# Layer A's attention: the transposes of the probabilities one step ahead of their products with the values

## The chip, the cores and the metric

The kernel runs on one core of a Trainium2 chip. The metric is the device time of one execution in microseconds (us), the median of several runs. The engines are TensorE (PE, with its weight loads as PEld), VectorE (DVE), ScalarE (ACT), GpSimd (POOL) and SyncE (SP), whose queue issues the DMAs here.

## What is computed

A trunk of two layers over 1024 positions of width 1024, in float32. Layer A is sparse attention: an indexer scores the keys, the 256 best admissible ones count, and 16 heads share one key and one value head. Then comes a squared-ReLU MLP, then layer B (latent attention) and a second MLP. The change touches layer A's attention alone. In the reference it is:

```python
def block(args):
    ...
    _, idx = lax.top_k(score, n_top)
    valid = (idx // CHUNK) <= t_chunk[None, :, None]
    kg = jax.vmap(lambda kk, ii: kk[ii])(k, idx)
    vg = jax.vmap(lambda vv, ii: vv[ii])(v, idx)
    logits = jnp.einsum('bqhd,bqkd->bhqk', qb, kg).astype(jnp.float32) * (A_HEAD_DIM ** -0.5)
    bias = rel_bias[t5_bucket(idx - t[None, :, None])]
    logits = logits + jnp.transpose(bias, (0, 3, 1, 2)).astype(jnp.float32)
    logits = jnp.where(valid[:, None], logits, NEG)
    p = jax.nn.softmax(logits, axis=-1).astype(vg.dtype)
    return jnp.einsum('bhqk,bqkd->bqhd', p, vg)
...
return out @ w_o
```

The kernel gathers nothing: it takes the logits of all admissible keys and adds a mask that is very negative where a key was not chosen.

## The kernel before

Positions are cut into eight blocks of 128, tb 0 to 7. `attend_a` runs twice, for the blocks (1, 3, 0, 2) at about 205 to 400 us and for (7, 4, 5, 6) at about 763 to 972 us. The first half of layer A's MLP lies between the two, its second half behind the second; layer B's attention follows at about 1345 to 1890 us, the last MLP to the end. Float32 products are made of two or three products of high and low parts (`split_evac`, line 88: ACT copies a PSUM tile to the high part, DVE or POOL subtracts it from the source for the low part).

A call's work is cut into units, one for a block and two heads (g, 0 to 7), 32 to a call. A unit has these steps:

- `logits` for each head (line 543: `lps`, two products per stretch of keys). Once a unit, SP loads the bias near the diagonal (`bm`, line 529, two buffers) and POOL adds the mask (line 530). DVE moves the logits to SBUF (`lg`), adds bias or mask and takes the running extreme (line 548, `sm`), ACT takes the exponential (552), DVE the reciprocal (553), POOL scales (554).
- `values` for two key blocks at a time: PE turns the probabilities (line 566, four transposes into a `ppt` tile), ACT and DVE split them into `ph` and `pl` (line 88), and PE multiplies those with the values `vv` into `po` (line 572). For each `ph`, `pl` and `ppt` there are two buffers in the first call; `ppt` has three in the second.
- `output`: ACT and DVE bring `po` to `res` (580 to 584).

Beside the units run: query projections (`pq`, line 185, blocks of 48 products), the query split and transposes (`qt`, `ptq`, line 515), the loading of the output weight (`load_wo`: eight times one DMA `wor_a`, ACT's `woh_a`, POOL's `wol_a`; a single `wor_a` buffer), and the output projections of the blocks that are done (`pwoa`, line 1066, two blocks of 24 products each, in a single PSUM buffer `pwo`; their residual add, line 1068).

The loop over k interleaves unit k's logits (`first`) with unit k-1's values (`second`), one step of each by turns, and strews the side work (`extra`) between; side work is tied behind the last transpose written before it (`self.anchor`). This program order is only a priority. A scheduler works out each engine's instruction order from it and from the buffers, and the engines then run their own lists strictly in that order.

Of the kernel before, what the change touches and what calls it, by code (L numbers as in the profile page):

```python
# [10 lines left out]
F32 = mybir.dt.float32  # L11
F32R = mybir.dt.float32r
# [6 lines left out]
P = 128  # L19
# [8 lines left out]
def woven(main, extra):  # L28

    steps, done = [], 0  # L30
    for i, step in enumerate(main):
        upto = (i + 1) * len(extra) // len(main)
        steps += [step] + extra[done:upto]
        done = upto
    return steps


def weave(main, extra, run=lambda e: e()):
    for step in woven(main, [lambda e=e: run(e) for e in extra]):
        step()  # L40


class Trunk:
# [433 lines left out]
    def attend_a(self, tbs, res, kh, kl, vv, score, edge, near_d, wst, lp=None, start=None, beside=None, free=None):  # L477
# [3 lines left out]
        nc, tc = self.nc, self.tc  # L481
        H, G = 16, 2
        wide = (max(tbs) + 1) * P
        nm0 = f"{tbs[0]}"
        with ExitStack() as st:
            qp = st.enter_context(tc.tile_pool(name="atq" + nm0, bufs=2))
            pp = st.enter_context(tc.tile_pool(name="atp" + nm0, bufs=2, space=PSUM))
            lp = lp or st.enter_context(tc.tile_pool(name="atl" + nm0, bufs=2, space=PSUM))
            queries, probs, outs = {}, {}, {}
# [30 lines left out]
            t2 = st.enter_context(tc.tile_pool(name="at2" + nm0, bufs=2))  # L520

            def logits(tb, g, i):
# [31 lines left out]
                nc.gpsimd.tensor_scalar(lg[:, :S], lg[:, :S], rs, 1.0, op0=ALU.mult, op1=ALU.mult)  # L554
                ps_h.append(lg)

            def values(tb, g, s0):
                nb = tb + 1
                if s0 == 0:
                    outs[tb, g] = pp.tile([P, G * P], F32, name=f"po{tb}_{g}", tag="po", bufs=2 if wide > 512 else 1)  # L560
                po, ps_h = outs[tb, g], probs[tb, g][2]
                ns = min(2, nb - s0)
                pt = pp.tile([P, 2, G, P], F32, name=f"ppt{tb}_{g}_{s0}", tag="pt", bufs=3 if wide > 512 else 2)
                for u in range(ns):
                    for i in range(G):
                        self.anchor = nc.tensor.transpose(pt[:, u, i], ps_h[i][:, (s0 + u) * P:(s0 + u + 1) * P], self.ident)  # L566
                ph = t2.tile([P, 2, G * P], F32R, name=f"ph{tb}_{g}_{s0}", tag="ph")
                pl = t2.tile([P, 2, G * P], F32R, name=f"pl{tb}_{g}_{s0}", tag="pl")
                self.split_evac(ph[:, :ns], pl[:, :ns], pt[:, :ns].rearrange("p u a b -> p u (a b)"))
                for u in range(ns):  # L570
                    for n, m in enumerate((ph, pl)):
                        nc.tensor.matmul(po, vv[:, s0 + u], m[:, u], start=(s0 + u == 0 and n == 0),  # L572
                                         stop=(s0 + u == nb - 1 and n == 1))

            def output(tb, g):

                po = outs.pop((tb, g))
                del probs[tb, g]
                of = t2.tile([P, P], F32, name=f"of{tb}_{g}", tag="of")
                nc.scalar.copy(of[0:64], po[64:128, 0:P])  # L580
                nc.scalar.copy(of[64:128], po[0:64, P:2 * P])
                dst = res[:, tb, g * P:(g + 1) * P]
                nc.vector.tensor_add(dst[0:64], po[0:64, 0:P], of[0:64])
                nc.vector.tensor_add(dst[64:128], po[64:128, P:2 * P], of[64:128])
# [6 lines left out]
            units = [(tb, g) for tb in tbs for g in range(H // G)]  # L591
            NU = len(units)

            def spread(steps, u0, u1):
                for n in range(u0, u1):
                    work[n] += steps[(n - u0) * len(steps) // (u1 - u0):(n - u0 + 1) * len(steps) // (u1 - u0)]


            work = [[] for _ in units]
# [7 lines left out]
            for k in range(NU + 1):  # L607
                if k == n0 + 1:
                    if free:
                        free()  # L610
                    wop = wst.enter_context(tc.tile_pool(name="awo" + nm0, bufs=1, side="right"))
                    wo, load = self.load_wo(wop, t1, self.d["a_w_o"][0], "a" + nm0)
                    spread(load, n0, n1)
                first = [lambda i=i: logits(*units[k], i) for i in range(G)] if k < NU else []
                second, extra = [], []
                if k:
                    tb, g = units[k - 1]
                    second = [lambda s0=s0: values(tb, g, s0) for s0 in range(0, tb + 1, 2)] + [lambda: output(tb, g)]
                    m = (k - 1 - n1) // each
                    if k > n1 and (k - 1 - n1) % each == 0 and m < 3:  # L620
                        spread(project(tbs[m]), k - 1, k - 1 + each)
                    extra = work[k - 1]
                steps = []
                for i in range(max(len(first), len(second))):
                    steps += second[i:i + 1] + first[i:i + 1]
                weave(steps, extra, self.behind)
            self.anchor = None

        def finish(tb, split, bank):
# [629 lines left out]
```

## Time and profile before

| | us |
|---|---|
| median of three runs | 2685.81 (2684.93 to 2688.6) |
| the profiled execution | 2684.85 |
| its span, first to last instruction | 2683.0 |
| PE busy within the span | 2532.4 |

The profiled execution lies 1 us below the median; 1.9 us of it are outside the span. Its mean granted clock is 0.984 of full speed. An engine's idle time is listed under what ended it, so a wait named "po <- DVE pl" is PE standing at a values product until DVE's subtraction was done.

### The profile page before, as it was taken

To read this page: it belongs to the slowest core of one execution; us is meant where nothing else is said; L and a number is where in the kernel's file an instruction comes from. 1 tells how busy PE (TensorE), PEld (TensorE's weight loads), DVE (VectorE), ACT (ScalarE), POOL (GpSimd) and SP (SyncE) were. 2 spreads that over 40 slices of the span, in tenths; PEclk is the share of its full clock that TensorE was granted. 3 is DMA by queue.
4 is the path that set the end of the run, shared out by engine and by line. 5 is a ranking of instruction groups with operands and counts; after the bars stand their busy time and mean duration, and the time that the engine had idled before them with its cause. 6 is when DMAs were issued, how large, how long until landed. Compare 5 with 4: busy or idle time off the path is not lost.

```text
span 2683.0 us, 36853 instructions
## 1 busy us (share of the span) xinstructions
PE 2532.4 (94%) x13354; PEld 2148.5 (80%) x13354; DVE 1521.1 (57%) x3655; ACT 1232.2 (46%) x2989; POOL 1024.1 (38%) x756
## 2 busy tenths in 40 slices
PE   6997799999989999999998999998999999999999
PEld 5897678888768888888888788887778888888887
DVE  5798754999869861222257878897422232222223
ACT  4575744333357764243345777787222222222221
POOL 2235635443556535343324555555121212222120
PEclk9998999999999999999999999999999999999999
DMA  7202323222232223233210000002210101111111
GB/s 157 54 24 60 99 92 97 94 99 90 79 110 68 60 82 127 84 120 106 77 33 11 10 14 10 14 5 80 102 32 32 63 32 63 47 48 48 48 47 63
DMA packets 122293, 173.03 MB, mean 64 GB/s; under 512 B 12752, under 2 KB 101104, under 8 KB 122112
## 3 DMA queue, kind: packets, MB, share of 16 engines
q1 hardware_dynamic: 122112, 170.69, 20.5%
q8 instruction: 105, 1.72, 0.3%
q14 instruction: 76, 0.62, 0.1%
HBM read 159.13 MB, written 11.53 MB: 64 GB/s over the span
## 4 chain that ended last, share of the span: by engine, by line
PE 71%; DVE 7%; DMA 3%; ACT 3%; POOL 2%; issue 2%; SPq 0%; POOLq 0%; DVEq 0%; ACTq 0%
PE pd L1190 25%; PE pu L1120 25%; PE pwo L1066 3%; PE pwoa L1066 2%; PE blps L938 2%; PE bpo L962 2%; PE puq L794 2%; PE po L572 1%; PE ppt L566 1%; PE lps L543 1%; PE pcq L853 1%; PE pukv L750 1%; DVE bpr L939 1%; PE bpt L957 1%; PE pck L853 1%
## 5 line engine op out<-in xcount | busy, mean ns | idle before, releaser
L88 POOL TENSOR_TENSOR dl<-rd,dh 128x1024 fp32r<-128x1024 f32 x96 | 232.4, 2429 | 728.2 <-PE pu L1120 369.3
L1191 DVE TENSOR_TENSOR res<-res,pd 128x1024 f32<-128x1024 f32 x192 | 234.2, 1220 | 419.1 <-PE pd L1190 419.1
L1120 PE MATMUL pu<-mxh,uh 128*128 128x512 f32 (+1 forms) x1056 | 405.4, 384 | 2.4 <-DVE mxl L88 2.4
L1120 PE MATMUL pu<-mxl,uh 128*128 128x512 f32 (+1 forms) x1056 | 404.9, 383 | 0.0
L1120 PE MATMUL pu<-mxh,ul 128*128 128x512 f32 (+1 forms) x1056 | 404.9, 383 | 0.0
L1190 PE MATMUL pd<-dh,hh 128*128 128x512 f32 x1024 | 398.6, 390 | 5.1 <-DVE res L1191 3.1
L1190 PE MATMUL pd<-dl,hh 128*128 128x512 f32 x1024 | 398.5, 389 | 0.0
L1190 PE MATMUL pd<-dh,hl 128*128 128x512 f32 x1024 | 392.9, 389 | 1.6 <-DVE hl L88 1.6
L88 DVE TENSOR_TENSOR hl<-pu,hh 128x512 fp32r<-128x512 f32 (+1 forms) x132 | 88.8, 674 | 407.6 <-ACT hh L88 407.6
L88 ACT CAST dh<-rd 128x1024 fp32r<-128x1024 f32 x96 | 99.1, 1051 | 476.1 <-PE pd L1190 422.5
L88 POOL TENSOR_TENSOR ul<-ru,uh 128x1024 fp32r<-128x1024 f32 x96 | 231.9, 2418 | 167.2 <-ACT uh L88 166.9
L1177 ACT ACTIVATE pu<-pu 128x512 f32<-128x512 f32 (+1 forms) x132 | 75.0, 569 | 433.2 <-PE pu L1120 427.7
L1120 PEld LDWEIGHTS pu<-mxh,uh 128*128 128x128 f32 x1056 | 199.1, 189 | 41.7 <-DVE mxl L88 2.9
L1120 PEld LDWEIGHTS pu<-mxl,uh 128*128 128x128 f32 x1056 | 198.9, 188 | 39.0
L1120 PEld LDWEIGHTS pu<-mxh,ul 128*128 128x128 f32 x1056 | 199.0, 188 | 38.7
L1190 PEld LDWEIGHTS pd<-dh,hh 128*128 128x128 f32 x1024 | 192.3, 188 | 46.5 <-DVE res L1191 4.0
L1190 PEld LDWEIGHTS pd<-dh,hl 128*128 128x128 f32 x1024 | 192.2, 188 | 42.1 <-DVE hl L88 2.2
L1190 PEld LDWEIGHTS pd<-dl,hh 128*128 128x128 f32 x1024 | 192.3, 188 | 39.7
L444 DVE TENSOR_SCALAR_CACHE_REDUCE both<-score,cand 128x1024 f32<-128x1024 f32 (+1 forms) x192 | 181.2, 944 | 5.0
L944 POOL TENSOR_SCALAR bpr<-bpr,bsm 128x640 f32<-128x640 f32 (+7 forms) x128 | 98.4, 772 | 96.4 <-DVE bsm L943 55.9
L554 POOL TENSOR_SCALAR lg<-lg,sm 128x256 f32<-128x256 f32 (+7 forms) x128 | 99.4, 783 | 76.7 <-DVE sm L553 54.0
L88 ACT CAST uh<-ru 128x1024 fp32r<-128x1024 f32 x96 | 99.9, 1044 | 30.4 <-DMA ru<-in_mlp_w_up_dram 28.4
(374 smaller groups left out, 5982.0 us busy)
## 6 DMA issues: line engine op xcount, KB each, us to landing
ru<-in_mlp_w_up_dram SPq DMA_DIRECT2D x48, 1024.0 KB, 5.4
rd<-in_mlp_w_down_dram SPq DMA_DIRECT2D x48, 1024.0 KB, 4.9
bm<-near_d SPq DMA_DIRECT2D x56, 256.0 KB, 2.7
res<-in_x_dram SPq DMA_DIRECT2D x16, 512.0 KB, 6.3
wor_a<-in_a_w_o_dram SPq DMA_DIRECT2D x16, 512.0 KB, 3.6
wr_q<-in_a_w_in_dram SPq DMA_DIRECT2D x8, 512.0 KB, 8.7
x<-res SPq DMA_DIRECT2D x8, 512.0 KB, 2.6
wor_b<-in_b_w_o_dram SPq DMA_DIRECT2D x8, 512.0 KB, 3.6
```

What stands on the lines that cost most here:

```text
L88: return self.nc.scalar.copy(h, src), (engine or self.nc.vector).tensor_sub(l, src, h)
L444: nc.vector.tensor_scalar(scratch[0][0][:, :s.shape[-1]], s, cand[:, j:j + 1], None, op0=ALU.is_ge, op1=ALU.add, accum_out=cnt[:, j:j + 1])
L554: nc.gpsimd.tensor_scalar(lg[:, :S], lg[:, :S], rs, 1.0, op0=ALU.mult, op1=ALU.mult)
L794: nc.tensor.matmul(ps[:, 192 * u:192 * u + 192], a[:, kb, tsl], b[:, kb], start=(kb == 0 and i == 0), stop=(kb == 2 and i == 2))
L853: nc.tensor.matmul(ps, a[:, kb], b[:, kb], start=(kb == 0 and i == 0), stop=(kb == KB - 1 and i == 2))
L938: nc.tensor.matmul(lps, q[0:rows, tsl], k[0:rows, h, c:c + a], start=(m == 0), stop=(m == 2))
L944: nc.gpsimd.tensor_scalar(pr, pr, sm[:, 3:4], 1.0, op0=ALU.mult, op1=ALU.mult)
L1066: nc.tensor.matmul(open_ps[n], x[:, kb], w[:, kb, ns], start=(kb == 0 and i == 0), stop=(kb == KB - 1 and i == 2))
L1120: nc.tensor.matmul(pu, a[:, kb], b[:, kb, c0:c1], start=(kb == 0 and i == 0), stop=(kb == KB - 1 and i == 2))
L1177: nc.scalar.activation(pu, pu, AF.Relu)
L1190: nc.tensor.matmul(pd[:, ns], a[:, tsl], b[:, ns], start=(f == 0 and k == 0), stop=(f == NS - 1 and k == 2))
L1191: nc.vector.tensor_add(res[:, tb], res[:, tb], pd)
```

## The change

`values` is cut in two. The new `turn_probs` makes the transposes and the split; `values` keeps the products. For a unit the order is now: the first transposes; then, for each step, the next step's transposes, a share of the following unit's logits with the side work between them, and the products of this step; the output last. `ph` and `pl` get three buffers each instead of two. The number of instructions is the same, and so is the work of each.

```diff
--- before.py
+++ after.py
@@ -554,21 +554,28 @@
                 nc.gpsimd.tensor_scalar(lg[:, :S], lg[:, :S], rs, 1.0, op0=ALU.mult, op1=ALU.mult)
                 ps_h.append(lg)
 
+            parts = {}
+
+            def turn_probs(tb, g, s0):
+                ps_h = probs[tb, g][2]
+                ns = min(2, tb + 1 - s0)
+                pt = pp.tile([P, 2, G, P], F32, name=f"ppt{tb}_{g}_{s0}", tag="pt", bufs=3 if wide > 512 else 2)
+                for u in range(ns):
+                    for i in range(G):
+                        self.anchor = nc.tensor.transpose(pt[:, u, i], ps_h[i][:, (s0 + u) * P:(s0 + u + 1) * P], self.ident)
+                ph = t2.tile([P, 2, G * P], F32R, name=f"ph{tb}_{g}_{s0}", tag="ph", bufs=3)
+                pl = t2.tile([P, 2, G * P], F32R, name=f"pl{tb}_{g}_{s0}", tag="pl", bufs=3)
+                self.split_evac(ph[:, :ns], pl[:, :ns], pt[:, :ns].rearrange("p u a b -> p u (a b)"))
+                parts[tb, g, s0] = ph, pl
+
             def values(tb, g, s0):
                 nb = tb + 1
                 if s0 == 0:
                     outs[tb, g] = pp.tile([P, G * P], F32, name=f"po{tb}_{g}", tag="po", bufs=2 if wide > 512 else 1)
-                po, ps_h = outs[tb, g], probs[tb, g][2]
-                ns = min(2, nb - s0)
-                pt = pp.tile([P, 2, G, P], F32, name=f"ppt{tb}_{g}_{s0}", tag="pt", bufs=3 if wide > 512 else 2)
-                for u in range(ns):
-                    for i in range(G):
-                        self.anchor = nc.tensor.transpose(pt[:, u, i], ps_h[i][:, (s0 + u) * P:(s0 + u + 1) * P], self.ident)
-                ph = t2.tile([P, 2, G * P], F32R, name=f"ph{tb}_{g}_{s0}", tag="ph")
-                pl = t2.tile([P, 2, G * P], F32R, name=f"pl{tb}_{g}_{s0}", tag="pl")
-                self.split_evac(ph[:, :ns], pl[:, :ns], pt[:, :ns].rearrange("p u a b -> p u (a b)"))
-                for u in range(ns):
-                    for n, m in enumerate((ph, pl)):
+                po = outs[tb, g]
+                hl = parts.pop((tb, g, s0))
+                for u in range(min(2, nb - s0)):
+                    for n, m in enumerate(hl):
                         nc.tensor.matmul(po, vv[:, s0 + u], m[:, u], start=(s0 + u == 0 and n == 0),
                                          stop=(s0 + u == nb - 1 and n == 1))
 
@@ -611,19 +618,25 @@
                     wop = wst.enter_context(tc.tile_pool(name="awo" + nm0, bufs=1, side="right"))
                     wo, load = self.load_wo(wop, t1, self.d["a_w_o"][0], "a" + nm0)
                     spread(load, n0, n1)
-                first = [lambda i=i: logits(*units[k], i) for i in range(G)] if k < NU else []
-                second, extra = [], []
+                other = [lambda i=i: logits(*units[k], i) for i in range(G)] if k < NU else []
                 if k:
                     tb, g = units[k - 1]
-                    second = [lambda s0=s0: values(tb, g, s0) for s0 in range(0, tb + 1, 2)] + [lambda: output(tb, g)]
                     m = (k - 1 - n1) // each
                     if k > n1 and (k - 1 - n1) % each == 0 and m < 3:
                         spread(project(tbs[m]), k - 1, k - 1 + each)
-                    extra = work[k - 1]
-                steps = []
-                for i in range(max(len(first), len(second))):
-                    steps += second[i:i + 1] + first[i:i + 1]
-                weave(steps, extra, self.behind)
+                    other = woven(other or [lambda: None], [lambda e=e: self.behind(e) for e in work[k - 1]])
+
+                    starts = list(range(0, tb + 1, 2))
+                    n = len(starts)
+                    steps = [lambda: turn_probs(tb, g, 0)]
+                    for i in range(n):
+                        if i + 1 < n:
+                            steps += [lambda s0=starts[i + 1]: turn_probs(tb, g, s0)]
+                        steps += other[i * len(other) // n:(i + 1) * len(other) // n]
+                        steps += [lambda s0=starts[i]: values(tb, g, s0)]
+                    other = steps + [lambda: output(tb, g)]
+                for step in other:
+                    step()
             self.anchor = None
 
         def finish(tb, split, bank):
```

The scheduler's lists differ in the first call from about 259 us on, in the whole second call, and also in layer B's attention, whose code is untouched; both MLPs stand as before. Three places follow. The names are those of the last section; digits behind a name are block and unit or head, then the first key block.

PE in the first call, at the query projection `pq3_6` of 48 products. Before:

```order
L572 MATMUL po3_1_3037<-ph3_1_2_3069,vv_75 128x256
L572 MATMUL po3_1_3037<-pl3_1_2_3070,vv_75 128x256
L185 MATMUL pq3_6_2847<-wh_q3_1970,axh1_105 128x256
L185 MATMUL pq3_6_2847<-wl_q3_1969,axh1_105 128x256
L185 MATMUL pq3_6_2847<-wh_q3_1970,axl1_107 128x256
```

and in the change:

```order
L565 MATMUL ppt3_3_0_3153<-ident_58,lg3_6_3117 128x128
L565 MATMUL ppt3_3_0_3153<-ident_58,lg3_7_3131 128x128
L543 MATMUL lps3_13_0_3322<-kh_73,qst3_2722 128x512
L543 MATMUL lps3_13_0_3322<-kl_74,qst3_2722 128x512
L185 MATMUL pq3_6_2854<-wh_q3_1970,axh1_105 128x256
L185 MATMUL pq3_6_2854<-wl_q3_1969,axh1_105 128x256
L185 MATMUL pq3_6_2854<-wh_q3_1970,axl1_107 128x256
```

Half a unit's transposes and one head's logits (`lps3_13`) now stand ahead of the projection, where they stood behind it. At the projection before, `pq3_4`, `lps3_8` moved the other way, from ahead of it to behind.

POOL in the first call, at the fourth of the eight `wol_a`. Before:

```order
L530 TENSOR_TENSOR bm0_4_3606<-bm0_4_3606,edge_83 128x2x128
L88 TENSOR_TENSOR wol_a1_2981<-wor_a1_3_3281,woh_a1_2982 128x1024
L554 TENSOR_SCALAR lg0_5_3531<-lg0_5_3531,sm0_2_3517 128x128
L554 TENSOR_SCALAR lg0_6_3562<-lg0_6_3562,sm0_3_3561 128x128
L554 TENSOR_SCALAR lg0_7_3582<-lg0_7_3582,sm0_3_3561 128x128
L530 TENSOR_TENSOR bm0_5_3666<-bm0_5_3666,edge_83 128x2x128
L554 TENSOR_SCALAR lg0_8_3610<-lg0_8_3610,sm0_4_3609 128x128
```

and in the change:

```order
L554 TENSOR_SCALAR lg0_3_3484<-lg0_3_3484,sm0_1_3475 128x128
L554 TENSOR_SCALAR lg0_4_3515<-lg0_4_3515,sm0_2_3514 128x128
L554 TENSOR_SCALAR lg0_5_3523<-lg0_5_3523,sm0_2_3514 128x128
L554 TENSOR_SCALAR lg0_6_3556<-lg0_6_3556,sm0_3_3555 128x128
L530 TENSOR_TENSOR bm0_4_3600<-bm0_4_3600,edge_83 128x2x128
L554 TENSOR_SCALAR lg0_7_3571<-lg0_7_3571,sm0_3_3555 128x128
L530 TENSOR_TENSOR bm0_5_3647<-bm0_5_3647,edge_83 128x2x128
L88 TENSOR_TENSOR wol_a1_2981<-wor_a1_3_3272,woh_a1_2982 128x1024
L554 TENSOR_SCALAR lg0_8_3604<-lg0_8_3604,sm0_4_3603 128x128
```

`wol_a` stands behind the scaling of heads 5 to 7 and the mask of `bm0_5`, which it stood ahead of. The others but the first move the same way by one to four instructions, the last by three (`lg2_8`, `lg2_9`, `bm2_6`). On SP, `wor_a` number 1, 2 and 4 to 7 (counted from 0) stand behind one or two more `bm` loads: the seventh behind `bm2_4`, the eighth behind `bm2_6`, which stood behind them before. On PE the last steps of `pwoa1_0`, the projection that takes up the weight as it arrives, have six transposes (`ppt2_4`), six products (`po2_3`) and one head's logits (`lps2_15`) ahead of them that stood behind them. At the call's end the last unit's products `po2_7` stand ahead of 48 `pwoa0` and 38 MLP products (`pwo`), where they stood right ahead of the transposes `pt_m` that need their result. Three `res` loads, where two did, stand ahead of the first MLP weight on SP.

DVE in the second call, at the query split of block 5. Before:

```order
L88 TENSOR_TENSOR qt5_8156<-res_69,qt5_8156 128x16x64
L88 TENSOR_TENSOR pl7_5_4_7612<-ppt7_5_4_7606,ph7_5_4_7611 128x512
L548 ISA lg4_0_7751,sm4_0_7750<-lps4_0_384_7756,bm4_0_7747,sm4_0_7750 128x256
L548 ISA sm4_0_7750 128x1
L88 TENSOR_TENSOR pl7_5_6_7625<-ppt7_5_6_7619,ph7_5_6_7624 128x512
```

and in the change:

```order
L88 TENSOR_TENSOR pl7_5_4_7583<-ppt7_5_4_7577,ph7_5_4_7582 128x512
L548 ISA lg4_0_7769,sm4_0_7768<-lps4_0_0_7770,score4_79 128x384
L548 ISA sm4_0_7768 128x1
L553 RECIPROCAL sm7_7_7676<-sm7_7_7676 128x1
L548 ISA lg4_0_7769,sm4_0_7768<-lps4_0_384_7774,bm4_0_7765,sm4_0_7768 128x256
L548 ISA sm4_0_7768 128x1
L88 TENSOR_TENSOR qt5_8172<-res_69,qt5_8172 128x16x64
L548 ISA lg4_1_7794,sm4_0_7768<-lps4_1_0_7795,score4_79 128x384
L548 ISA sm4_0_7768 128x1
L88 TENSOR_TENSOR pl7_5_6_7608<-ppt7_5_6_7602,ph7_5_6_7607 128x512
```

`pl7_5_4`, which the next values product needs, stands six instructions ahead of `qt5`; before it stood right behind. In several units of block 5 the transposes of three tiles now follow one another on PE, with up to six `pwoa` products behind them; before, four transposes and three `pwoa` took turns. Over the second call's PE list a transpose is followed by something else 130 times, before 123 times.

## Rows read from the trace of the kernel before

**Rows 1.** The page's busy time of each engine, share of the span, instructions.

```profile
PE 2532.4 (94%) x13354; PEld 2148.5 (80%) x13354; DVE 1521.1 (57%) x3655; ACT 1232.2 (46%) x2989; POOL 1024.1 (38%) x756
```

**Rows 2.** Stretches: us; PE, PEld, DVE, ACT, POOL busy (instructions); PE clock; DMA share, GB/s.

```profile
270.00:350.00 80.00, 61.05 (x377) 49.63 (x377) 60.01 (x244) 57.32 (x157) 58.26 (x64) 0.96 0.35 103
330.00:350.00 20.00, 15.14 (x82) 11.00 (x83) 15.84 (x70) 15.05 (x42) 18.81 (x20) 1.00 0.44 132
350.00:400.00 50.00, 47.40 (x239) 38.78 (x238) 25.27 (x65) 20.05 (x43) 10.16 (x10) 1.00 0.22 76
763.00:820.00 57.00, 47.19 (x291) 38.61 (x290) 50.65 (x160) 44.39 (x80) 44.55 (x32) 0.94 0.35 104
820.00:970.00 150.00, 145.64 (x986) 131.12 (x985) 133.17 (x416) 110.16 (x242) 77.45 (x72) 1.00 0.18 50
1445.00:1890.00 445.00, 404.81 (x2614) 347.41 (x2611) 364.80 (x1117) 337.04 (x1097) 242.68 (x254) 0.97 0.07 21
```

**Rows 3.** PE's waits, 259 to 400 us: line <- releaser: total us, times, longest.

```profile
PE lps L543 <- DVE sm L548: 4.4, 4, 1.9
PE po L572 <- DVE pl L88: 2.6, 4, 1.1
PE ptq L515 <- DVE pl L88: 2.1, 1, 2.1
PE ppt L566 <- DVE pl L88: 1.6, 4, 1.1
PE pt_m L116 <- DVE res L584: 1.3, 1, 1.3
```

**Rows 4.** Timeline, loading of the output weight: start us, us, engine, line, operation [idle before].

```profile
287.10 2.39 POOL L88 TENSOR_TENSOR wol_a<-wor_a,woh_a 128x1024 fp32r<-128x1024 f32 x1
330.42 0.35 SPq L1045 DMA_DIRECT2D wor_a<-in_a_w_o_dram  x1
334.15 1.04 ACT L88 CAST woh_a<-wor_a 128x1024 fp32r<-128x1024 f32 x1 [0.65 <-DMA wor_a<-in_a_w_o_dram]
336.91 2.39 POOL L88 TENSOR_TENSOR wol_a<-wor_a,woh_a 128x1024 fp32r<-128x1024 f32 x1
344.10 2.41 POOL L88 TENSOR_TENSOR wol_a<-wor_a,woh_a 128x1024 fp32r<-128x1024 f32 x1
344.60 3.38 SPq L529 DMA_DIRECT2D bm<-near_d  x2
```

**Rows 5.** Groups of 290 to 400 us: count | busy us, mean ns | idle before.

```profile
L88 DVE TENSOR_TENSOR pl<-ppt,ph 128x512 fp32r<-128x512 f32 x16 | 10.9, 688 | 2.1 <-ACT ph L88 2.0
L88 ACT CAST ph<-ppt 128x512 fp32r<-128x512 f32 x15 | 8.7, 582 | 5.9 <-PE po L572 4.3 <-PE ppt L566 1.5
```

**Rows 6.** Timeline around DVE's query splits (columns as in rows 4).

```profile
813.83 2.38 POOL L88 TENSOR_TENSOR wol_a<-wor_a,woh_a 128x1024 fp32r<-128x1024 f32 x1
814.39 2.90 DVE L88 TENSOR_TENSOR qt<-res,qt 128x1024 fp32r<-128x1024 f32 x1
817.94 0.39 PE L572 MATMUL po<-pl,vv 128*128 128x256 f32 x1 [2.66 <-DVE pl L88]
302.86 1.22 DVE L88 TENSOR_TENSOR qt<-res,qt 128x1024 fp32r<-128x1024 f32 x1
304.26 2.38 POOL L88 TENSOR_TENSOR wol_a<-wor_a,woh_a 128x1024 fp32r<-128x1024 f32 x1 [2.28 <-ACT woh_a L88]
```

**Rows 7.** Timeline of PE in the second call: successive instructions.

```profile
866.31 0.29 PE L572 MATMUL po<-pl,vv 128*128 128x256 f32 x1
866.43 0.60 PE L566 MATMUL ppt<-ident,lg 128*128 128x128 f32 x4
866.79 0.48 PE L1066 MATMUL pwoa<-woh_a,oh 128*128 128x512 f32 x1
867.11 0.40 PE L1066 MATMUL pwoa<-wol_a,oh 128*128 128x512 f32 x1
867.34 0.40 PE L1066 MATMUL pwoa<-woh_a,ol 128*128 128x512 f32 x1
```

## The prediction, made before the changed kernel ran

> **What bounds the kernel now.** I read the page's busy times first, then the stretches of the two calls, then PE's waits in the part that the order changes, and last the timeline of what those waits hang on. PE is busy 94% of the span [rows 1], so only PE's idle time within the changed stretches can be won, and no more than that. The second call has little of it: from 820 to 970 us PE is busy 145.64 of 150 us and DVE 133.17; only its start, 763 to 820 us, stands 57 - 47.19 = 9.8 us, part of it the entry that the change does not touch. The first call has more: 80 - 61.05 = 19 us from 270 to 350 us, while from 350 to 400 us PE runs almost without a gap (47.40 of 50). From 330 to 350 us POOL is the fullest, 18.81 of 20 us [rows 2]. So there are two regimes in the first call: up to about 348 us PE waits for others, behind it PE sets the end.
>
> The waits from 259 us on are of two kinds. Those that the change aims at end with DVE's `pl`: at a product 2.6 us, at a turned query 2.1 (one wait), at a probability transpose 1.6, together 6.3 us. The others, 4.4 us at the logits alone, end with DVE's reduction [rows 3]. The split that PE waits for takes 0.58 us on ACT and then 0.69 on DVE [rows 5]; a transpose group followed at once by its products pays both.
>
> What sets the point where PE becomes dense is the output weight. A step of its loading took 334.15 - 330.42 = 3.73 us from issue to ACT, 1.04 on ACT and 2.39 on POOL, 7.16 together; the single `wor_a` buffer lets the next begin only then. The eight ran from 287.10 to 344.10 us, 57.0/7 = 8.14 us apart [rows 4]. Only with the last one can the first projection's half finish its sums, and since the projections share one PSUM buffer, all that follows is PE work that waits for nothing else.
>
> **The change part by part.** No instruction is added; what moves is counted here, against the profiled execution (2684.85 us, span 2683.0). It lies 0.96 us under the median, so I add the difference to the median, 2685.81.
>
> *First call, lead of the attention.* With the transposes a step ahead, the next transposes and logits lie between a split and its products, and half a unit stands ahead of the 48-product block `pq3_6`, so ACT, DVE and POOL have work during it. I count half of the 6.3 us as gone, 3.15, because in the same lists `lps3_8` moved behind a block of that length, and since a shorter wait for `pl` shows the one for the logits behind it. The bounds are 0 and 6.3. Moving the last `wol_a` behind `bm2_6` gives the attention another 2.41 us of POOL in the stretch where POOL is full. Lead near 344 us: 3.15 + 2.41 = 5.6 us (0 to 8.7).
>
> *First call, the weight.* What is moved past it costs here. The last `wor_a` DMA now stands on SP behind the load of `bm2_6`, which before was issued at 344.60 us, as it waits for a bias buffer. At an unchanged pace the last `wol_a` would start at 344.60 + 0.35 + 3.73 + 1.04 = 349.7 instead of 344.10 us [rows 4], 5.6 us late. The lead of 5.6 us cancels it: term 0, bounds -5.9 (seven steps of 7.16 us from 287.10 make 337.2; with a step of queueing left I take 338.2) and +5.6. So the chain that ends the first regime is not shortened by my sum, and most of the 19 us stay, moved only to other places.
>
> *First call, less left behind the weight.* Six transposes and six products more are done ahead of the last `pwoa1_0` steps. Four transposes take 0.36 us to the next start and a product 0.12 [rows 7]: 6 x 0.09 + 6 x 0.12 = 1.3, with one head's two logits products, which I take as two of 0.12, 1.5 us: -1.5. If the weight were not last, this would be worth nothing: bounds -1.5 and 0.
>
> *First call, the tail.* The last unit's products now stand 86 products ahead of the transposes that need them, 86 x 0.23 = 20 us of cover [rows 7], so the 1.3 us wait for `res` goes [rows 3]. In its place two halves of a projection follow each other on one PSUM buffer with nothing between: the adding out, a DVE operation of the width of `pl`, 0.69 us [rows 5]. -1.3 + 0.7 = -0.6. Of the other 50 - 47.40 - 1.3 = 1.3 us of idle time there I take 0.5 as gone. The MLP weight behind a third `res` load starts some us later; the same cover, 20 us where there were 12, hides it, and without it its delay would be paid in full at the first MLP products. Tail: -1.1 (-2.6 to +2).
>
> *Second call.* PE is dense, so nothing but its few waits can be won. The longest is 2.66 us at 817.94 us, a product waiting for `pl`. DVE was then at the query split `qt`, 2.90 us, while POOL ran `wol_a` from 813.83 us; at 302.86 us, with POOL idle until 304.26, the same split took 1.22 [rows 6]. In the new list the awaited `pl7_5_4` stands ahead of `qt5`, and behind it is work that PE needs one or two products later. I take half of the stall: -1.3 (-2.66 to 0). The price: a transpose followed by something else occurs seven times more often, and the first start behind a transpose group is 0.32 us away against 0.23 between products of the same width [rows 7], 7 x 0.09 = +0.6. Three tiles turned at once want three splits of DVE in a row, 3 x 0.69 = 2.1 us [rows 5]; six `pwoa`, 6 x 0.23 = 1.4 us, and the third buffer cover them but for 0.7 us, and no unit's products wait for all three. Second call: -0.7 (-3.5 to +4, the upper end if in six of the eight units of block 5 the 0.7 us is paid).
>
> The Trainium skill, page "SBUF — State Buffer", section "Who interferes with whom", says that a DVE instruction with two SBUF inputs contends with a GpSimd instruction that reads SBUF, and one with at most one such input does not. The two rows of `qt` (both inputs in SBUF) agree with it. By that rule the split stays 2.9 us long wherever a `wol_a` meets it, and the term would be 0 instead of -1.3, the sum +1.3 higher.
>
> *Layer B.* Its lists differ through the scheduler alone. It idles 445 - 404.81 = 40.2 us [rows 2]; I take 0, with a tenth of that, 4 us, either way.
>
> Sum: 0 - 1.5 - 1.1 - 0.7 + 0 = -3.3 us; 2685.81 - 3.3 = **2682.5 us**.
>
> **The rivals.** *A larger gain.* The lead grows to its upper end, and the weight no longer queues: -5.9 - 1.5 - 1.1 in the first call, -2.0 in the second: -10.5, about 2675. For it: 6.3 us end with `pl`, and DVE has room (60 of 80 us from 270 to 350). Against: POOL is at 94% where the chain ends, and the logits' waits are untouched.
>
> *The change does nothing.* A wait for `pl` becomes one for the logits or for POOL's scaling at the next instruction; lead 2.4 us only, the weight +3.2, less left -1.5, tail -1.1, second call -0.7: 2685.7. For it: PE, DVE and POOL are all used in turn, and a list in strict order only passes a stall on.
>
> *Slower: the output weight behind the attention.* The `wor_a` DMAs stand behind `bm` loads that wait for buffers, and one buffer chains the eight. With no lead the last `wol_a` is 5.6 us late, the 1.5 us less behind it are won, the tail pays its 0.7 us, the second call its 0.6: +5.4, 2691.2. It decides from a lead under about 3 us near 344 us. For it: the weight's places on both queues; against: those 2.41 us of POOL are freed for certain.
>
> **How the numbers follow.** A measurement of this kernel can tell about 0.2%, 5.4 us, from no change: faster ends at 2680.4, slower begins at 2691.2. Chances: my forecast 0.45 (2677 to 2686 by its terms), the larger gain 0.20, nothing 0.18, slower 0.17 with half of it at or above 2691.2, and layer B adds its 4 us to the upper side of some others. Below 2680.4 lie the larger gain and two fifths of the forecast: 0.20 + 0.18 = 0.38. Above 2691.2 I put 0.14; between them 0.48. The range for 8 in 10 goes from 2673 to 2691.
>
> **What would show it.** In the changed trace: the last `wol_a` of the first call near 344 us (338 for the larger gain, 348 and more for the slower case); the three waits with `pl` at half of 6.3 us between 259 and 400 us; the wait for `res` ahead of `pt_m` gone and one of about 0.7 us between two projections; PE dense behind the weight as before; the stall at about 818 us halved; layer B within 4 us. The forecast is wrong if the weight's loading moves by more than 3 us, or if the second call, dense as it is, loses time at the grouped transposes.

## The result

The change is slower: 2702.64 us (six executions, 2694.24 to 2704.06) against 2685.4 before, a ratio of 1.0055 [1.0044, 1.0065] (in brackets its 95% interval; the two medians alone make 1.0064). Run again (e1), the ratio is 1.0061 [1.0046, 1.0076]. The prediction was 2682.5 us, and its range ended at 2691. The profiled execution of the change is the shortest of the six: 2694.24 us, span 2692.2, 9.2 us over the span before. So a trace of it accounts for 9 of the 17 us between the medians; e1 below has a longer one.

The stretches of [rows 2] in the change (us; PE, PEld, DVE, ACT, POOL busy; PE clock; DMA share, GB/s):

```profile
270.00:350.00 80.00, 63.07 (x378) 50.67 (x377) 60.84 (x250) 57.34 (x162) 59.91 (x67) 0.96 0.33 97
330.00:350.00 20.00, 14.79 (x81) 10.86 (x80) 15.87 (x68) 14.53 (x40) 15.78 (x17) 1.00 0.26 84
350.00:400.00 50.00, 42.97 (x203) 33.88 (x201) 19.46 (x36) 15.26 (x29) 7.13 (x6) 0.98 0.30 97
763.00:820.00 57.00, 49.06 (x294) 37.69 (x294) 48.26 (x154) 44.16 (x78) 44.49 (x31) 0.94 0.39 121
820.00:970.00 150.00, 139.89 (x942) 124.23 (x941) 130.47 (x408) 104.21 (x233) 76.33 (x71) 1.00 0.18 50
1445.00:1890.00 445.00, 405.44 (x2662) 348.39 (x2662) 369.97 (x1134) 340.71 (x1131) 244.06 (x256) 0.98 0.07 21
```

From 270 to 350 us PE does 2 us more than before, and from 763 to 820 as well; PE's work in layer B (1445 to 1890) is within 1 us. From 350 to 400 us, where nothing should have been in its way, it is busy 42.97 us instead of 47.40, and in the second call 139.89 instead of 145.64.

PE's waits from 259 to 412 us, answering to [rows 3] (line <- releaser: total, times, longest):

```profile
PE pt_m L116 <- DVE ms_m L78: 4.7, 1, 4.7
PE lps L543 <- DVE sm L548: 4.1, 7, 1.4
PE ptq L515 <- DVE qst L516: 3.4, 3, 2.4
PE po L579 <- ACT ph L88: 2.1, 2, 1.6
PE ppt L565 <- DVE pl L88: 1.4, 2, 1.0
PE po L579 <- DVE pl L88: 0.6, 2, 0.3
```

The waits for `pl` fell from 6.3 to 2.0 us: at products to 0.6, at transposes to 1.4, at the turned query to none. But products now wait 2.1 us for ACT's `ph`, and the turned query 3.4 us for `qst`, two waits that the trace before does not list, so little of the 4.3 us is PE time won. A new wait of 4.7 us stands ahead of the MLP's transposes `pt_m`. The timeline around it (start, us, engine, line, operation [idle before]):

```profile
341.32 2.38 POOL L88 TENSOR_TENSOR wol_a<-wor_a,woh_a 128x1024 fp32r<-128x1024 f32 x1 [0.94 <-ACT woh_a L88]
381.69 0.33 SPq L126 DMA_DIRECT2D g_mlp<-in_mlp_norm_dram  x1
381.77 1.06 ACT L96 ACTIVATE xq<-res 128x1024 f32<-128x1024 f32 x1 [10.69 <-PE pwoa L1079]
382.44 0.47 PE L1079 MATMUL pwo<-woh_a,mxh 128*128 128x512 f32 x1 [0.83 <-issue]
386.17 2.48 DVE L106 SCALAR_TENSOR_TENSOR xs_m<-res,y_m,g_mlp 128x1024 f32<-128x1024 f32 x2 [0.50 <-DMA g_mlp<-in_mlp_norm_dram]
390.80 2.00 ACT L88 CAST uh<-ru 128x1024 fp32r<-128x1024 f32 x2 [6.83 <-DMA ru<-in_mlp_w_up_dram]
391.38 1.91 PE L116 MATMUL pt_m<-ident,xs_m 128*128 128x128 f32 x16
391.93 4.73 POOL L88 TENSOR_TENSOR ul<-ru,uh 128x1024 fp32r<-128x1024 f32 x2 [6.84 <-ACT uh L88]
393.65 1.07 ACT L96 ACTIVATE xq<-res 128x1024 f32<-128x1024 f32 x1
396.62 0.56 POOL L81 TENSOR_TENSOR y_m<-ms_m,mhalf 128x1 f32<-128x1 f32 x1
398.86 1.28 DVE L106 SCALAR_TENSOR_TENSOR xs_m<-res,y_m,g_mlp 128x1024 f32<-128x1024 f32 x1
400.29 1.94 PE L116 MATMUL pt_m<-ident,xs_m 128*128 128x128 f32 x8 [4.68 <-DVE ms_m L78]
401.88 0.56 PE L1133 MATMUL pu<-mxh,uh 128*128 128x256 f32 x1
```

The last `wol_a` is 2.8 us earlier than before [rows 4], and the first product of the last projection (`pwo`) comes at 382.44 instead of 388.21 us. But the MLP's gain `g_mlp` is loaded at 381.69 us, ACT's first norm of the MLP (`xq`) begins at 381.77 after a wait of 10.69 us for PE's `pwoa`, and DVE scales at 386.17 once the gain has landed. The wait at `pt_m` itself is for the third block: its norm (`xq`) begins on ACT at 393.65, behind the weight's `uh`, which had waited 6.83 us for the DMA of `ru`, and then queues on POOL behind the weight split `ul` (4.73 us). Before, the first two norms were long done, the third stood ahead of `uh` and `ul`, and 16 of the `pt_m` transposes stood ahead of the first `pwo`:

```profile
208.30 0.47 SPq L126 DMA_DIRECT2D g_mlp<-in_mlp_norm_dram  x1
356.90 1.06 ACT L96 ACTIVATE xq<-res 128x1024 f32<-128x1024 f32 x1
370.68 1.06 ACT L96 ACTIVATE xq<-res 128x1024 f32<-128x1024 f32 x1
386.51 1.94 PE L116 MATMUL pt_m<-ident,xs_m 128*128 128x128 f32 x16 [1.34 <-DVE res L584]
388.21 0.48 PE L1066 MATMUL pwo<-woh_a,mxh 128*128 128x512 f32 x1
388.31 1.07 ACT L96 ACTIVATE xq<-res 128x1024 f32<-128x1024 f32 x1
390.17 0.55 POOL L81 TENSOR_TENSOR y_m<-ms_m,mhalf 128x1 f32<-128x1 f32 x1 [17.26 <-DVE ms_m L78]
392.43 2.00 ACT L88 CAST uh<-ru 128x1024 fp32r<-128x1024 f32 x2 [2.00 <-issue]
400.35 0.28 PE L1120 MATMUL pu<-mxh,uh 128*128 128x256 f32 x1
```

The first MLP product comes at 401.88 us, 1.5 us later than before (400.35), though the first `pwo` had been 5.8 us early: the stretch between the two, called the tail below, grew by 7.3 us. Of these, 1.7 us are the 16 transposes (386.51 to 388.21 us before), which now stand inside the stretch; 5.6 us are lost, 4.7 in the wait and the rest in products behind it at the lower clock level (last section). In the second call PE waits more for POOL's scaling of the probabilities. From 820 to 985 us, in the change:

```profile
PE ppt L565 <- POOL lg L554: 6.1, 9, 1.4
PE lps L543 <- DVE sm L548: 1.8, 4, 1.0
```

and before:

```profile
PE ppt L566 <- POOL lg L554: 2.0, 2, 1.0
PE lps L543 <- DVE sm L548: 0.4, 2, 0.2
```

From the call's first query transposes (764.49 us; before 760.46) to the first MLP product behind it (1001.41; before 990.34) it takes 236.9 us instead of 229.9. So the 9.2 us are -5.8 + 7.3 + 2.5 in the MLP between the calls (part of it the stretch at the lower clock level) + 7.0 in the second call - 1.9 from there to the end, layer B included.

### The profile page after: what moved, and what is told of

Read it like the earlier page. It is cut to its first block, busy times and chain, and to the rows that moved or that the text cites. A ratio compares the mean times of both kernels' runs of the same rounds, so it can differ in the third digit from the quotient of the medians.

```text
span 2692.2 us, 36799 instructions
## 1 busy us (share of the span) xinstructions
PE 2534.6 (94%) x13354; PEld 2143.0 (80%) x13354; DVE 1521.6 (57%) x3655; ACT 1229.4 (46%) x2989; POOL 1022.6 (38%) x756
## 4 chain that ended last, share of the span: by engine, by line
PE 74%; DVE 13%; ACT 4%; DMA 4%; POOL 3%; issue 2%; SPq 0%; POOLq 0%; DVEq 0%; ACTq 0%
PE pd L1203 25%; PE pu L1133 25%; PE pwo L1079 3%; PE blps L951 2%; PE pq L185 2%; PE puq L807 2%; PE pwoa L1079 2%; PE bpo L975 2%; DVE lg L548 1%; PE po L579 1%; PE ppt L565 1%; PE pukv L763 1%; PE pqi L172 1%; PE pcq L866 1%; DMA bm<-near_d 1%
## 5 line engine op out<-in xcount | busy, mean ns | idle before, releaser
L552 ACT ACTIVATE lg<-lg,sm 128x256 f32<-128x256 f32 (+7 forms) x128 | 99.6, 779 | 39.0 <-DVE sm L548 31.7
```

What stands on the lines that cost most here:

```text
L552: nc.scalar.activation(lg[:, :S], lg[:, :S], AF.Exp, bias=mn, scale=-1.0, accum_out=sm)
```

## The experiments

Each difference is against the kernel before or the change, and shortened to the lines that matter; `ahead` chooses for each call between the new order and the old one. The table stands ahead because the experiments are read from it: all from one profiled execution each, the ratio from the timed ones and executions of the kernel before timed beside them. "Tail" runs from the first `pwo` product to the first MLP product; "second" as just told.

| kernel | last wol_a | first pwo | tail | second call | ratio to before |
|---|---|---|---|---|---|
| before | 344.10 | 388.21 | 12.14 | 229.9 | |
| the change | 341.32 | 382.44 | 19.44 | 236.9 | 1.0055 |
| e1 the change again | 343.84 | 386.17 | 19.07 | 237.6 | 1.0061 |
| e2 old order, three buffers, both calls | 343.88 | 385.03 | 19.11 | 234.9 | 1.0035 |
| e3 new order, three buffers, first call | 346.82 | 389.03 | 18.93 | 231.7 | 1.0024 |
| e4 new order, three buffers, second call | 343.68 | 387.82 | 12.14 | 235.8 | 1.0018 |
| e5 before, room taken in first call | 340.48 | 383.88 | 19.28 | 230.7 | 1.0031 |
| e6 new order, two buffers | 349.52 | 391.56 | 12.14 | 229.9 | 0.9993 |
| e7 the same, first call alone | 353.40 | 395.47 | 12.14 | 228.5 | 1.0001 |
| e8 the same, second call alone | 344.20 | 388.33 | 12.15 | 234.0 | 0.9992 |
| e9 old order, three buffers, second call | 343.80 | 387.91 | 12.14 | 239.6 | 1.0018 |
| e10 new order, two buffers, weight earlier | 330.20 | 379.65 | 12.14 | 232.9 | 0.9960 |
| e11 old order, two buffers, weight earlier | 333.32 | 387.31 | 13.18 | 234.8 | 1.0013 |
| e12 new order, third pl for a fifth lg | 341.55 | 397.28 | 13.30 | 228.8 | 1.0015 |
| e13 before, room taken in second call | 344.34 | 388.49 | 12.14 | 233.5 | 1.0008 |
| e14 new order, third buffers in first call | 344.86 | 387.21 | 19.89 | 236.1 | 1.0040 |
| e15 new order, third buffers in second call | 348.76 | 390.87 | 12.14 | 237.9 | 1.0042 |

How far does one execution carry? In the second call the lists of before, or almost these, take 228.5 to 233.5 us (before, e3, e5, e7, e13); those of the new order with two buffers, but for a few places, 228.8 to 236.1 (e6, e8, e12, e14); those of the change 235.8 to 237.9 (the change, e1, e4, e15). So a single second call is known to within some 7 us only. The first call's lists of before bring the last `wol_a` at 340.48 to 344.34 us (before, e4, e5, e8, e9, e13), and from the second call's end to the end of the span the kernels take 1685.4 (e6) to 1692.7 us (before). The tail is steadier: 12.14 or 12.15 in nine kernels, 18.93 to 19.89 in the six in which the gain is loaded late, and 13.2 to 13.3 in e11 and e12, with products at the lower clock level.

**e1, the change again.**

> The change once more, on the chip of the three kernels that follow. Its profiled execution took 2694.24 us, its other executions 2701 to 2704 us at a lower mean clock (0.980 to 0.982 against 0.985). If the difference belongs to the kernel, this run lies again at 2694 to 2704 us, and a profile of the longer kind shows where the clock falls: one theory puts it at the stall of 4.7 us ahead of the MLP's transposes pt_m near 400 us, the rival in the second call or layer B, spread over many short waits.

2702.74 us. The profiled execution took 2699.11; its tail and second call lose what the first profile showed, so the loss belongs to the kernel. Its span is 14.0 us over the one before: the first MLP product is 4.9 us later, the MLP between the calls takes 3.1 more, the second call 7.7 more, the rest 1.7 less. The executions of 2701 us and more were not profiled, and what they lose beyond this is open. What separates e1 from the first profile is mainly a first call with a smaller lead, part of it at the lower clock level: from 330 to 350 us the granted clock is 0.83 on the mean, where the first profile has 1.00.

```profile
330.00:350.00 20.00, 15.52 (x75) 12.40 (x75) 13.53 (x61) 13.09 (x37) 17.58 (x19) 0.83 0.35 105
```

**e2, three buffers alone.** The old order, and

```diff
-tag="ph")
-tag="pl")
+tag="ph", bufs=3)
+tag="pl", bufs=3)
```

> The order of before with three ph and three pl buffers in both calls, nothing else. Theory one: the third buffers take the room in SBUF in which the MLP's gain and the scratch of its first norm stood early, so both wait for the end of the attention; then the gain's load is issued only after about 380 us here too, PE stands 3 to 8 us around 385 to 402 us, and the kernel takes 2689 to 2694 us. Rival: the tail's loss comes from the order of the last products alone; then this kernel is at 2685 us, give or take 2.

2696.12 us, 1.0035 [1.0024, 1.0046]: theory one by its signs, and 2.1 us above its range. The tail takes 19.11 us with the old order of the last products, so their order is not the cause.

**e3 and e4, one call at a time.**

```diff
+ahead = wide <= 512     # e3; e4: wide > 512
-bufs=3
+bufs=3 if wide <= 512 else 2     # e4: wide > 512
```

> The new order and the third buffers in the first call alone, the second call as before. Theory one: the last wol_a starts about 341 us as in the change, and the tail loses its 8 us, so the first MLP product is at 401 to 403 us and the kernel at 2687 to 2692 us. Theory two, that the second call's grouped transposes cost the larger part, agrees with that and puts the rest of the change's loss, 7 us or more, there. Rival, that the first call alone causes all: 2694 us or more.

> The new order and the third buffers in the second call alone, the first as before. Theory two: PE idles about 5 us more from 820 to 960 us than before, as in the change (there 10.1 of 150 us against 4.4), and the kernel takes 2690 to 2694 us. Rival: the second call loses only because it starts in another state after the first; then 2685 us, give or take 3, with the idle time of before.

2692.15 us (1.0024 [1.0010, 1.0039]) and 2690.95 us (1.0018 [1.0006, 1.0031]). Both calls lose; e3's profile has the tail, though not the earlier weight that I expected (346.82 us). Of e4's pair, theory two holds and the rival does not: the second call loses behind an unchanged first.

**e5, the room alone.** The kernel before, with

```diff
+if wide <= 512:
+    t2.tile([P, 1024], F32, name="pad" + nm0, tag="pad", bufs=1)
```

> The kernel before, two ph and two pl buffers, the old order, with 4 KB a partition of SBUF set aside unused beside them in the first call: as much as a third ph and pl take. Theory one (room): the MLP's gain is loaded only near 383 us and ACT's first norms of the MLP wait for the end of the last projection; the time goes to 2689 to 2693 us, 4 to 7 over before, all of it between 370 and 412 us. Rival: the third buffers cost by what they let run ahead; then this kernel is at 2686 us, give or take 2, like before.

2694.75 us, 1.0031 [1.0017, 1.0045]. The instruction lists differ from those of before only in the MLP's gain, its norms and the tail, and in layer B. In the timeline the gain's load stands where the change has it:

```profile
382.96 0.33 SPq L126 DMA_DIRECT2D g_mlp<-in_mlp_norm_dram  x1
```

and PE waits ahead of `pt_m`:

```profile
PE pt_m L116 <- DVE ms_m L78: 2.9, 1, 2.9
```

A second wait, 2.3 us, stands ahead of the first `pwo`, where before 1.3 us stood ahead of `pt_m`. So 4 KB a partition, used for nothing, delay the MLP's norms to the end of the last projection and cost about 8 us, a little over the 7 that I gave it at most. That is the first half of the loss.

**e6, e7, e8, the new order with two buffers**, in both calls, in the first, in the second:

```diff
-bufs=3
+bufs=2
```

> The change in both calls with two ph and two pl buffers. Theory one: the gain is loaded at about 208 us as before, the wait of 4.7 us ahead of pt_m is gone, the first MLP product comes at 393 to 397 us (before 400.4, change 401.9), and the kernel is 8 to 12 us faster than the change: 2690 to 2695 us; what stays over before is the second call. Rival, that the order and not the room costs: within 3 us of the change's 2702.6.

> The new order in the first call alone, with two buffers; second call as before. If the first call's lead (the last wol_a near 341 us instead of 344) is real and the room was what spoiled it, the first MLP product comes 3 to 6 us earlier than before and the kernel takes 2680 to 2684 us: the form that could beat before. Rival, that the lead needs the third buffer or is given back at the projections: 2686 us, give or take 2.

> The new order in the second call alone, with two buffers. Theory two (in the second call the transposes, moved ahead, now wait for POOL's scaling of their own probabilities, and a third buffer lets them move further ahead): these waits fall from the 6 us of the second call alone with three buffers to 2 to 4, and the kernel takes 2687 to 2690 us. Rival, that the grouped transposes and DVE's splits in a row cost: as with three buffers, 2690 to 2692 us.

2685.21 (0.9993 [0.9984, 1.0002]), 2686.35 (1.0001 [0.9990, 1.0013]) and 2685.0 us (0.9992 [0.9982, 1.0001]): the order by itself does nothing that can be measured in the time, and the whole loss hangs on the third buffers. In the first call it does lose: the first MLP product comes at 403.70 us in e6, where I expected 393 to 397, and at 407.61 in e7, against 400.35 before, because the weight came late. In e6's profile the time behind the second call, 7.3 us shorter than before, makes up for it; layer B's lists differ there too, and why it is shorter is open. The waits for `pl` from 259 to 412 us are not shortened by the order alone; in e6 they are 6.3 us in all, as before:

```profile
PE ptq L515 <- DVE pl L88: 3.0, 3, 2.1
PE ppt L565 <- DVE pl L88: 2.2, 4, 1.1
PE po L579 <- DVE pl L88: 1.1, 2, 0.8
```

The weight's last split, in e6:

```profile
349.52 2.37 POOL L88 TENSOR_TENSOR wol_a<-wor_a,woh_a 128x1024 fp32r<-128x1024 f32 x1
```

That is 5.4 us behind the 344.10 of before, and near the 349.7 that the prediction worked out for an unchanged pace (e7 has 353.40, e15 348.76). The first `pwo` product then follows 42.04 us behind it where it was 44.11; 0.5 us of that is a shorter wait for `res` ahead of `pt_m` (0.87 against 1.34), the other 1.6 is less work left.

**e9, the third buffer in the second call alone, old order**

```diff
-bufs=2
+bufs=3 if wide > 512 else 2
```

> The old order with three ph and pl buffers in the second call alone; the first call is as before. Theory: the third buffer by itself, through the lists that the scheduler makes with it, costs the second call 4 to 7 us there, with PE's wait for POOL's scaled probabilities at 4 to 6 us instead of 2 from 820 to 985 us; the kernel takes 2689 to 2693 us. Rival, that in the second call the loss needs both, the new order and the third buffer: 2686 us, give or take 2.

2692.22 us, 1.0018 [1.0009, 1.0028], as the theory had it. PE's waits from 820 to 985 us:

```profile
PE ppt L565 <- POOL lg L554: 8.6, 6, 2.5
PE lps L543 <- DVE sm L548: 0.7, 2, 0.4
```

8.6 us instead of 2.0, and more than the 4 to 6 expected. With e13 (below) this is the second half: not room but the lists made with the third buffer. In the new order this wait is 6.1 to 6.4 us in all four kernels that have the third buffer in the second call, and 3.3 to 5.0 in the five that have two. From e15 and from e6:

```profile
PE ppt L565 <- POOL lg L554: 6.2, 9, 1.4
PE ppt L565 <- POOL lg L554: 3.5, 4, 1.4
```

**e10 and e11, the weight earlier.** Two buffers; the side work is tied behind the transposes of one step before, which moves the weight's loads ahead of bias loads. e10 has the new order, e11 the old.

```diff
+self.anchor = turned[-1] if turned else self.anchor
 for u in range(ns):
     for i in range(G):
-        self.anchor = nc.tensor.transpose(...)
+        last = nc.tensor.transpose(...)
+turned.append(last)
```

> The new order in both calls with two buffers, and the side work tied behind the transposes of one step earlier, which puts the output weight's loads ahead of more bias loads on SP (the eighth behind bm2_3, before bm2_5, with the new order and two buffers bm2_5 or later). Theory: with two buffers the first call loses because the last wol_a came 5 us late (349.5 and 353.4 us against 344.1); here it starts at 338 to 343 us, and the kernel takes 2677 to 2683 us, faster than before. Rival, that the weight's end doesn't set the first call's: 2684 to 2687 us as with two buffers alone.

> The old order, two buffers, with the same earlier tie of the side work: the weight's loads stand as in the kernel just above. If the weight alone sets the end of the first call, this one gains as much as the kernel above over before: 2679 to 2684 us. If the new order's lead is needed for it, it stays at 2684 to 2688 us.

e10 takes 2675.19 us, 0.9960 [0.9948, 0.9973]: the fastest kernel here, below what I expected of it, and faster than both kernels of this study. e11 takes 2689.64 us, 1.0013 [1.0004, 1.0022], above both of its ranges. Both have the weight early; in e10:

```profile
330.20 2.38 POOL L88 TENSOR_TENSOR wol_a<-wor_a,woh_a 128x1024 fp32r<-128x1024 f32 x1 [1.05 <-ACT woh_a L88]
```

and in e11:

```profile
333.32 2.39 POOL L88 TENSOR_TENSOR wol_a<-wor_a,woh_a 128x1024 fp32r<-128x1024 f32 x1
```

In the old order the first MLP product does not move (400.49 us against 400.35): 10.8 us of lead in the weight are used up before it. In the new order it comes at 391.79. This reads as if the weight were one bound of the first call and the attention's own pace the other, close behind it; the new order relieves the second, the earlier weight the first, and only both together show. That both are needed is shown by the four times (before, e6, e11, e10); the reason is not, since the tie moves all side work, the projections too, and the weight's loads were not moved by themselves.

**e12, a third `pl` paid for by an `lg`.** New order; in the first call two `ph`, three `pl`, and four `lg` instead of five, so that the room is that of before; two buffers in the second.

> The new order in both calls, two ph, three pl in the first call, and four lg buffers there instead of five, so that the room in SBUF is that of before; second call with two buffers. Theory one (room): the gain is loaded at about 208 us again and no wait of 3 us or more stands ahead of pt_m. The time itself rests on how much four lg buffers hold the logits back: 2680 to 2690 us. Rival: a third buffer costs the tail whatever the room; then the wait ahead of pt_m is there and the time over 2692 us.

2691.17 us, 1.0015 [1.0004, 1.0025]. The gain is loaded at 208.33 us and the wait for the norm is gone, as theory one says; but the attention is later (first `pwo` at 397.28 us, though the last `wol_a` comes at 341.55), by the four `lg` as I read it. A bad trade.

**e13, room in the second call.** The edit of e5 for `wide > 512`.

> The kernel before with 4 KB a partition set aside unused in the second call; every engine's list reads as before. Theory: in the second call the third buffer costs by the lists made with it, not by its room, so this kernel is at 2685.5 us, give or take 2. Rival, that the room costs there too: 2689 us or more.

2687.02 us, 1.0008 [0.9999, 1.0017]: no measurable difference, with lists equal to those of before. Its interval overlaps that of e9, so the time alone does not set the two apart; what does is the wait that grew in e9, which from 820 to 985 us stays as before:

```profile
PE ppt L568 <- POOL lg L557: 2.0, 2, 1.1
```

**e14 and e15, do the halves add up?** The new order in both calls, the third buffers in the first or in the second.

> The new order in both calls, the third buffers in the first call alone. If the two parts of the loss add up, this is the kernel with two buffers everywhere (2685) plus the room's 8 us less the lead that the third buffers give: 2690 to 2695 us. Rival, that the change's loss stands only with third buffers in both calls: 2688 us or less.

> The new order in both calls, the third buffers in the second call alone. If the parts add up: two buffers everywhere (2685) plus the second call's 5 to 7 us, 2690 to 2692 us, with the gain loaded at about 208 us. Together with the kernel just above it should account for the change's 2702.6 to within 4 us; if the two excesses over 2685 sum to less than 13, something acts only with both, and stays open.

2697.54 (1.0040 [1.0024, 1.0057]) and 2695.85 us (1.0042 [1.0027, 1.0057]), 2.5 and 3.9 us over what I expected. Over e6 they lose 12.3 and 10.6 us, together 23, where the change loses 17.4. So nothing is missing; rather some 5 us are counted twice. The profiles hint where: e14 has almost e6's lists in the second call, and yet takes 236.1 us there where e6 takes 229.9, near the 237.9 of e15. With a scatter of 7 us in this stretch that is a hint only, so the halves stand as parts, not as prices that add up: the third buffers cost 6 us in each call alone (e3 against e7, e4 against e8) and 11 to 12 in this pair.

## Why the prediction was wrong

*The lead* was right in size but not in cause, and by luck. I gave half of it to the order and half to POOL. The change's waits for `pl` shrank by 4.3 of 6.3 us, inside the bounds, but waits for `ph` and `qst` took their place, much as the rival of no effect had it, and the order alone (e6) leaves the 6.3 us as they were. The last `wol_a` moved by -2.8 us (-0.3 in e1) where the sum had 0; kernels with the first call's lists of before differ by more. With the order and two buffers it is 5 to 9 us late (e6, e7, e15), and with three 341.3 to 346.8 us (the change, e1, e3, e14): the lead that cancels the weight's new places on the queues comes with the third buffers. That was the slower rival's mechanism, and it does occur, but in the times of e6 and e7 it nets to no change.

*Less left behind the weight*: -1.5 predicted, -1.6 in e6. In the change the first `pwo` follows the last `wol_a` by 41.12 us against 44.11, but most of that is the 16 transposes and the wait for `res` that are gone from this place; without these and the 0.8 us wait ahead of `pwo` it is -0.8.

*The tail* is the step that failed: -1.1 predicted, +5.1 measured. The wait for `res` went (-1.3), and 0.8 us stand in its place, as forecast; the other +5.6 are the wait ahead of `pt_m` and the slower products behind it. I counted 86 products of cover ahead of `pt_m` and charged the third buffers nothing. Their price was room: the scheduler's SP list had the gain's load moved from early in the first call to its end, and I weighed the `res` load beside it, not this one. With it the norms of two finished blocks were held back to 381.77 us, and the third block's norm came behind the weight's split instead of ahead of it, so the chain from norm to scaling to transposes began behind the cover instead of under it. Of the 86 products, the 38 `pwo` were no cover won by the order: they stand ahead of the transposes because these had become late, in the old order too (38 in e2, 39 in e5), and in e6 the transposes are ahead of the first `pwo` again. e5 shows the cause alone.

*The second call* is the second step that failed: -0.7 predicted, +7.0 measured, beyond the +4 of its bounds; over all profiles with the change's lists there (four) and those of before (five) the means differ by 6.2 us. The stall at 818 us did go; its place is taken by waits of 0.83 and 0.76 us for `ph`. Grouped transposes cost nothing by themselves in the time (e8). What I had as cover, the third buffer, is what lost: with it PE's list takes transposes up before POOL has scaled their probabilities, and a list runs strictly in order (e9, e15). That the releaser is POOL is shown; which places of the list cost most was not tried.

*Layer B*: 0 predicted with 4 us either way; from the second call's end to the end of the span -1.9 measured.

*The chances* left 0.14 for a time above 2691.2 us, mainly for one mechanism that turned out neutral. No rival rested on the buffers, the only resource that the change adds.

## What to carry to other kernels

An added buffer is paid for in room, and the bill may come in the next stage: look in the list for a load or a first operation of that stage that has moved, and follow what waits for it. Time an order without its extra buffers first, since a scheduler's list with more buffers can also run a strictly ordered engine into waits. Where two bounds lie close together, easing either shows nothing (e6, e11), and easing both can (e10). And where the same lists take 228.8 to 236.1 us in four kernels, as in the second call here, one profile does not tell a loss of 6 us: the timed executions and several profiles do.

## What was not expected of the hardware

After the 4.7 us wait the granted clock shows a stretch at the lower level, 1.2 GHz: the mean from 396 to 406 us is 0.66 in the change and 1.00 before, and the 32 `pt_m` transposes from 388 to 416 us take 310 ns on the mean (single ones 445) where the trace before has 273. It is the same behind the other waits of this kind (0.81 in e1, 0.83 in e2 and in e5 over the same 10 us; in e3, where the wait ends at 406 us, 1.00 over these 10 us and 0.66 from 405 to 410), and 1.00 in e6, where the wait is absent. So here the stall of PE is paid a second time in the products behind it. The fall does not belong to this one wait, though: e12, which lacks it, has two waits of 1.4 and 1.3 us for `res` close together and then 0.52 from 395 to 400 us. Columns as in the first table of stretches; the change:

```profile
396.00:406.00 10.00, 5.71 (x33) 5.74 (x34) 5.91 (x14) 2.32 (x4) 1.73 (x3) 0.66 0.33 105
```

and e5, which has only the room:

```profile
396.00:406.00 10.00, 7.05 (x41) 6.33 (x40) 7.81 (x17) 4.67 (x9) 1.33 (x3) 0.83 0.35 105
```

The query split of DVE that took 2.90 us beside a `wol_a` before [rows 6] took 1.23 in the change, and this time POOL's mask, begun 10 ns later, was the longer one: 2.36 us instead of 1.30.

```profile
815.32 1.30 POOL L530 TENSOR_TENSOR bm<-bm,score 128x512 f32<-128x512 f32 x1
820.46 1.23 DVE L88 TENSOR_TENSOR qt<-res,qt 128x1024 fp32r<-128x1024 f32 x1
820.47 2.36 POOL L530 TENSOR_TENSOR bm<-bm,score 128x512 f32<-128x512 f32 x1 [1.65 <-DVE sm L548]
```

The Trainium skill, page "SBUF — State Buffer", section "Who interferes with whom", says that the order of issue decides which of the two blocks; both traces agree with it, with DVE second and blocked in the one, POOL in the other.
